# Exchanging the order of the grouped-attention projections in a hybrid encoder trunk

## The chip, the cores and the metric

The kernel runs on one core of a Trainium2 chip. The metric is the device time of one execution in microseconds, the median of several runs. The engines of the core work at the same time, each through a queue of its own in the order of the program: TensorE (PE, matmuls and transposes), VectorE (DVE), ScalarE (ACT), GpSimd (POOL) and SyncE (SP, which only starts transfers here). An instruction that waits for another engine holds up everything behind it in its own queue.

## What is computed

Two layers over 512 prompt tokens and 256 sample tokens of width 1024. Cut to what matters:

```python
def _layer(x, c, ...):
    hid = _rms_norm(x, norm_g) * (1.0 + scale) + shift
    qa, ka, va, za, qb, kb, vb, zb, ga, gb = split(hid @ w_in)
    oa = _neighbourhood_attention(qa, ka, va, rpb)       # 8 heads of 64
    ya = (oa * silu(za)) @ w_pa
    qh = _axial_rope(_rms_norm(qb, q_norm_g))            # 8 query heads of 64
    kh = _axial_rope(_rms_norm(kb, k_norm_g))            # 2 key heads of 64
    ob = _gqa_attention(qh, kh, vb)
    yb = (ob * silu(zb)) @ w_pb
    g_a, g_b = split(sigmoid(concat([ga, gb]) + b_gate))
    return x + gate * ((g_a * ya + g_b * yb) @ w_out)
```

## The kernel before

**Numbers.** Every float32 operand of a matmul is split into a high part (rounded, on ACT) and a low part (the rest, on DVE), and a product is three matmuls: high by high, low by high, high by low. Weights come as tiles of 128 x 1024 (`raw`, from `wst`, in the order in which they are used) and are split by `split_one` into `whi` and `wlo` (lines 222 and 228); `ahead` splits the first tiles of the next chunk of weights during the present one, and `need_unit` calls whatever split is still open.

**Steps.** All work inside a layer is written as a list of steps (`step`, line 153). A step issues a group of matmuls: six over 512 columns or twelve over 256. Then the step counter goes up, the functions that were put off to this number with `defer` are issued, and after them, from the list `slots`, as many entries as the rate allows: `rate[0]` is added to a credit at every step, and each whole credit issues one entry. The order of every engine's queue is thus fixed by hand: matmuls of the step, deferred work, slots.

**Attention in slots.** Attention is spread over the projections' steps. A neighbourhood head (`na_slots`, line 747) covers 17 slots and the heads start 8 slots apart; a head's transposes of its sample probabilities and its prompt product are in its slot 10, its sample product in slot 14. A grouped head (`gqa_slots`, line 885) covers 24 slots, and the heads start 12 apart, 108 slots in all. In a grouped head, counted from its first slot: scores of five tiles at slots 0, 2, 4, 6, 8; the row maximum one slot later on DVE (`gss`, line 915), the exponential two later on ACT (`gp`, line 925), the division three later (a reciprocal on DVE, line 937, then a product on POOL, line 939). The probabilities are transposed by PE into `gtp` (line 950) at slots 7, 8, 12, 13 and 17 and read out by ACT and DVE (lines 712, 717).

**Order of chunks in a layer.** The list `order` (line 1006): `va`, four `pair` chunks (queries and keys of two neighbourhood heads each), then `qb` (grouped queries, 24 steps) and `kvb` (grouped keys and values, 12 steps), then `za` (two chunks), four times `ga` and `pa`, then the same for branch B and the output projection. From the fourth `pair` on, the remaining neighbourhood slots are spread over `RQ` = 31 steps. At the end of `qb` and `kvb` any left are issued at once.

**Between the pairs and `za`.** At line 1302 the gains and the rotation table are loaded (`gn`, `tr`), and four products on DVE (line 1310) make from them one table of two halves for queries, `tabs[0]`, and one for keys, `tabs[1]`. A projection's result is squared and copied out by ACT (`rope_part`, lines 1323 and 1324), summed by DVE one step later (line 1327, `qss`) and rotated by POOL two steps later (lines 1332 to 1336). `rope_finish` (line 1342) takes the inverse roots by Newton steps on DVE, twelve small operations in two consecutive steps (lines 1350 to 1369, `ny`, `na`), and from the second step after multiplies them in (line 1363, `rr`).

While `roping[0]` is true, the neighbourhood heads' division runs on DVE (line 796) instead of POOL.

The constants in `SC` place what follows, in steps: `QF`, `QT`, `QTT` set when the roots of the prompt's queries are taken and when their four transposes (`q_tr_p`, `qt`, line 1391) start after the fourth query tile's read-out, and how far they are apart; `QS` and `QST` the same for the sample's (`q_tr_s`, line 1404). `KF` and `KT` count from the end of `kvb`: roots of the keys (`kfin`), transposes of the prompt's keys (`ktr(0)`, `kt`, line 1444), and, two steps on, of the sample's (`ktr(1)`). Each transposed tile is read out of PSUM by ACT (high part, `GQ` at line 680 or `GK` at lines 688 and 689) and by DVE one step later (low part, lines 681, 692, 693); for keys the second head one step after the first. All transposes, the attention's too, go through the PSUM pool `ps_t`, which has two buffers (line 78).

`kv_evac` (line 1419) also writes the values' table `vg`: two pairs of a high part on ACT and a low part on DVE. `vg` comes from the pool `vp`, which has two buffers, held until then by the neighbourhood values of heads 0 to 3 and 4 to 7.

`SGQ` steps after the end of the projections `start_gqa` (line 1519) puts the 108 slots into the list, at `len(slots) / SC["RG"]` a step. What is left of them when branch B begins is issued at once (line 1533).

Of the kernel before, what the change touches and what calls it, by code (L numbers as in the profile page):

```python
# [7 lines left out]
F32 = mybir.dt.float32  # L8
# [27 lines left out]
    RN=11.6,  # L36
    RQ=31,

    QF=4,
    QT=10,  # L40
    QTT=2,
    QS=5,
    QST=13,
    KF=5,
    KT=12,
    SGQ=15,
    RG=84,

    SR0=90,
    SR1=40,  # L50
# [10 lines left out]
def trunk(ctx: ExitStack, tc: tile.TileContext, xT, xq, wst, wad, wsd, vec, gain, trig, mask, eye, rpb, yT):  # L61
# [49 lines left out]
    def pitch(ap):  # L111
        return ap.ap[0]
# [8 lines left out]
    def galloc(shape, dtype, name):  # L121
        tag = free.pop(0)
        t = genp.tile(shape, dtype, tag=tag, name=name)
        owner[id(t)] = (tag, t)
        return t

    def gfree(t):
        tag, _ = owner.pop(id(t))
        free.append(tag)
# [12 lines left out]
    def defer(k, fn):  # L142
        later.setdefault(step_no[0] + k, []).append(fn)
# [540 lines left out]
    def evac_k(Kh, Kl, hp, src, sl):  # L684
        p0 = 64 * hp
        p1 = 64 - p0
        h = Kh[p0:p0 + 64, sl]
        A.activation(out=h, in_=src[p0:p0 + 64], func=AF.Copy)
        A.activation(out=Kh[p1:p1 + 64, sl], in_=src[p0:p0 + 64], func=AF.Copy)

        def low():
            V.tensor_sub(out=Kl[p0:p0 + 64, sl], in0=src[p0:p0 + 64], in1=h.bitcast(F32))
            V.tensor_sub(out=Kl[p1:p1 + 64, sl], in0=src[p0:p0 + 64], in1=h.bitcast(F32))

        defer(1, low)
# [51 lines left out]
    def na_slots(l, h, base, Q, Kh, Kl, v4, dst, on_done, first):  # L747
# [95 lines left out]
            st["o"] = o  # L843

        def pv_s():
            o = ps_o.tile([128, NP], F32, tag="o", name="os")
            n = 0
            for b in range(2):
                for pt in st["pt", 2]:
                    mm(o[:, 0:256], v4[:, 4 + b, hi4, :], pt[:, b, :], n == 0, n == 3)  # L850
                    n += 1
            st["o"] = o
# [136 lines left out]

    bms = {}  # L990
    roping = [False]
    GQ = []
    GK = []
    slots_abs = []
# [11 lines left out]
    for l in range(DEPTH):  # L1006
        order += [("va", l)]
        order += [("pair", l, p) for p in range(4)]
        order += [("qb", l), ("kvb", l)]
        order += [("za", l, 0), ("za", l, 1)]  # L1010
        for i in range(4):
            order += [("ga", l, i), ("pa", l, i)]
        order += [("zb", l, 0), ("zb", l, 1)]
        for i in range(4):
            order += [("gb", l, i), ("pb", l, i)]
        order += [("wo", l, i) for i in range(4)] + [("wor", l, i) for i in range(2)]
# [5 lines left out]
    def nxt(name):  # L1022
        assert todo.pop(0) == name, name

    with tc.manual_schedule():
# [213 lines left out]
        for l in range(DEPTH):  # L1239
# [19 lines left out]
            slots_abs.clear()  # L1259
            pushed[0] = 0  # L1260
            slot_base = 0
            rate[0] = 16 / SC["RN"]
            bms[l, 0] = bm_build(l, 0)
            for p in range(4):
# [38 lines left out]
            S.dma_start(out=gn, in_=gain[l].unsqueeze(0).to_broadcast([128, 4, 64]))  # L1303
            tr = galloc([128, 6, 2, 64], F32, "tr")
            S.dma_start(out=tr, in_=trig)
            tabs = []
            for w in range(2):
                tb = galloc([128, 6, 2, 64], F32, "tab")
                for s in range(2):
                    V.tensor_mul(out=tb[:, :, s, :], in0=tr[:, :, s, :],  # L1310
                                 in1=gn[:, 2 * w + s].unsqueeze(1).to_broadcast([128, 6, 64]))
                tabs.append(tb)
            gfree(gn)
            gfree(tr)

            GQ[:] = [None] * 8
            GK.clear()
# [1 line left out]
            def rope_part(src, tab, r, ss):  # L1319

                n, nh = src.shape[1], src.shape[2]
                sq = galloc([128, n, nh, 64], F32, "rsq")
                A.activation(out=sq, in_=src, func=AF.Square)
                A.activation(out=r, in_=src, func=AF.Copy)

                def part2():
                    V.tensor_reduce(out=ss, in_=sq, axis=AX.X, op=ALU.add)

                def part3():
                    for e in range(2):  # L1330
                        sb = tab[:, :, 1, 32 * e:32 * e + 32].unsqueeze(2)
                        G.tensor_mul(out=sq[:, :, :, 32 * e:32 * e + 32], in0=r[:, :, :, 32 - 32 * e:64 - 32 * e],
                                     in1=sb.to_broadcast([128, n, nh, 32]))
                    cb = tab[:, :, 0, :].unsqueeze(2).to_broadcast([128, n, nh, 64])
                    G.tensor_mul(out=r, in0=r, in1=cb)
                    G.tensor_add(out=r, in0=r, in1=sq)
                    gfree(sq)

                defer(1, part2)
                defer(2, part3)  # L1340

            def rope_finish(rs, ss):
# [18 lines left out]
                for i, r in enumerate(rs):  # L1361
# [2 lines left out]
                        out=r, in0=r, in1=yv[:, t:t + k, :].unsqueeze(3).to_broadcast([128, k, nh, 64])))  # L1364
                    t += k

            nxt(("qb", l))
            roping[0] = True
            qr = {}
            qss = smp.tile([128, 6, 8], F32, tag="qss8", name="qss", bufs=1)  # L1370

# [26 lines left out]
            def q_tr_s(w):  # L1398
# [9 lines left out]
                if w == 1:  # L1408
                    for j in (4, 5):
# [1 line left out]

            wide_pass(("qb", l), [(0, 1), (2,), (3,), (4, 5)], q_evac,
                      lambda i: ps_acc.tile([128, NP], F32, tag="acc", name="accw"))
            nxt(("kvb", l))
            kr = galloc([128, 6, 2, 64], F32, "rr")
            kss = smp.tile([128, 6, 2], F32, tag="qss2", name="qss", bufs=1)
            vg = vp.tile([128, 6, 4, 128], F32R, tag="v", name="vg")

            def kv_evac(b, acc):
                rope_part(acc[:, :, 0:128].rearrange("p t (h d) -> p t h d", d=64), tabs[1][:, 2 * b:2 * b + 2],  # L1420
                          kr[:, 2 * b:2 * b + 2],
                          kss[:, 2 * b:2 * b + 2, :])
                base = vg[:, 2 * b:2 * b + 2]
                pp = pitch(base)
                src = acc[:, :, 128:256].rearrange("p t (k d) -> p t k d", d=64)
                for e in range(2):
                    hi = bass.AP(base.tensor, base.offset + 192 * e, [pp, [512, 2], [256, 2], [1, 64]])
                    lo = bass.AP(base.tensor, base.offset + 64 + 64 * e, [pp, [512, 2], [256, 2], [1, 64]])
                    A.activation(out=hi, in_=src, func=AF.Copy)
                    V.tensor_sub(out=lo, in0=src, in1=hi.bitcast(F32))  # L1430

            token_chunk(("kvb", l), kv_evac)
            roping[0] = False

            def kfin():
                rope_finish([kr[:, 0:4], kr[:, 4:6]], kss)

            def ktr(g):
                c, n = RNG[g]
                if g == 0:  # L1440
                    GK.extend([[galloc([128, NT], F32R, "GK") for _ in range(2)] for _ in range(2)])
                t = ps_t.tile([128, n], F32, tag="t", name="kt")
                for j in range(n // 128):
                    T.transpose(t[:, 128 * j:128 * j + 128], kr[:, 4 * g + j].rearrange("p h d -> p (h d)"), ident)
                evac_k(GK[0][0], GK[0][1], 0, t, slice(c, c + n))
                defer(1, lambda: evac_k(GK[1][0], GK[1][1], 1, t, slice(c, c + n)))
                if g == 1:
                    gfree(kr)
                    gfree(tabs[1])

            defer(SC["KF"], kfin)
            defer(SC["KT"], lambda: ktr(0))
            defer(SC["KT"] + 2, lambda: ktr(1))


            oaz = {}
# [44 lines left out]
            for h in range(8):  # L1501
                if h % 2 == 0:
                    pr = h // 2

                    def alloc_ob(pr=pr):
                        ob[pr] = galloc([128, NT], F32, "ob")
                    while len(slots_abs) <= 12 * h:
                        slots_abs.append([])
                    slots_abs[12 * h].insert(0, alloc_ob)

                def gdn(h=h):
                    gfree(GQ[h])
                    if h % 4 == 3:
                        gfree(GK[h // 4][0])
                        gfree(GK[h // 4][1])

                gqa_slots(12 * h, h, vg, ob, gdn)

            def start_gqa():
                push_slots()  # L1520
# [202 lines left out]
def _layout(inputs):  # L1723
# [33 lines left out]
    for l in range(DEPTH):  # L1757
        w = w_in[l]
        st += wide(w[:, va])
        for p in range(4):  # L1760
            st += halves(np.concatenate([cols(w, qa, p, 128), cols(w, ka, p, 128)], axis=1))
        st += wide(hperm(w[:, qb]))
        st += halves(np.concatenate([hperm(w[:, kb]), w[:, vb]], axis=1))
        for i in range(2):
            st += halves(cols(w, za, i))
        for i in range(4):
            st += halves(cols(w, ga, i))
            st += halves(g["w_pa"][l][:, 256 * i:256 * i + 256])
        for i in range(2):
            st += halves(cols(w, zb, i))  # L1770
        for i in range(4):
            st += halves(cols(w, gb, i))
            st += halves(g["w_pb"][l][:, 256 * i:256 * i + 256])
        for i in range(4):
            st += halves(g["w_out"][l][:, 256 * i:256 * i + 256])
        st += st[-8:-4]
# [80 lines left out]
```

## Time and profile before

| | before |
|---|---|
| median of 3 runs | 1226.61 us (1225.98 to 1226.78) |
| the profiled execution | 1225.67 us |
| its span, first to last instruction | 1223.9 us |
| ACT busy | 579.7 us (47%) |
| POOL busy | 342.9 us (28%) |
| mean granted TensorE clock | 0.997 |

The span is what the profile's rows add up in; the rest of the execution's time lies around it. In a row of the timeline stand the start, the duration, the engine, the line, the operation, `written<-read`, the shapes and a count; in brackets the idle time before it and what ended it. Busy time of PE is modelled at the ends of matmuls, which overlap, so a matmul's share is read from the distance of starts. In a row of windows stand the stretch, its length, and the busy time of PE, PEld (weight loads), DVE, ACT and POOL with instruction counts, then the granted clock, the DMA engines' share and GB/s.

### The profile page before, as it was taken

How to read it: one execution, taken by the hardware profiler on the slowest of the kernel's cores; microseconds unless marked ns; L12 is line 12 of the kernel's file. 1: busy time of each engine (PE TensorE's matmuls, PEld its weight loads, DVE VectorE, ACT ScalarE, POOL GpSimd, SP SyncE). 2: the span in 40 equal slices, each digit the busy share in tenths (PEclk: the TensorE clock that was granted, in tenths of full speed). 3: DMA queues.
4: the chain of work that ended last, by engine and by line, in shares of the span. 5: the costliest groups of instructions: out<-in, count | busy, mean ns of one | idle time of the engine just before them, and what ended most of it. 6: DMA issues, size and time to landing. Idle time of an engine off the chain costs nothing.

```text
span 1223.9 us, 19495 instructions
## 1 busy us (share of the span) xinstructions
PE 1202.9 (98%) x7276; PEld 1056.5 (86%) x7276; DVE 816.6 (67%) x1609; ACT 579.7 (47%) x1229; POOL 342.9 (28%) x382
## 2 busy tenths in 40 slices
PE   8999999999999999999999999999999999999997
PEld 5789989889898988887888998898898998888886
DVE  5757887875556458998484788777656554763536
ACT  4547755465555332433154676555545543332323
POOL 0025454442223121121131443554222212211102
PEclk9999999999999999999999999999999999999998
DMA  9443411111111235566443233111111112431424
GB/s 344 150 126 86 118 55 52 52 52 36 35 36 52 70 105 154 174 185 197 139 151 109 75 92 109 35 48 57 31 40 53 36 52 87 146 95 52 129 95 155
DMA packets 48125, 118.28 MB, mean 97 GB/s; under 512 B 5408, under 2 KB 11936, under 8 KB 48032
## 3 DMA queue, kind: packets, MB, share of 16 engines
q1 hardware_dynamic: 47888, 116.98, 30.9%
q8 instruction: 57, 0.93, 0.3%
q14 instruction: 36, 0.29, 0.1%
q10 hardware_dynamic: 144, 0.07, 0.0%
HBM read 110.74 MB, written 6.29 MB: 96 GB/s over the span
## 4 chain that ended last, share of the span: by engine, by line
PE 81%; DVE 10%; ACT 4%; issue 2%; DMA 2%; POOL 0%; SPq 0%; DVEq 0%; ACTq 0%; POOLq 0%
PE accp L115 37%; PE accs L115 19%; PE accw L115 9%; PE go L115 3%; PE gsp L115 3%; PE gtp L950 3%; PE acct L115 2%; DVE wlo L228 2%; ACT p L788 1%; PE sp L115 1%; DVE GQ L681 1%; DMA adaraw<-in_wad 1%; PE op L115 1%; PE adat L115 1%; DVE ptl L717 1%
## 5 line engine op out<-in xcount | busy, mean ns | idle before, releaser
L115 PE MATMUL accp<-hh,whi 128*128 128x512 f32 x512 | 203.4, 397 | 0.0
L115 PE MATMUL accp<-hl,whi 128*128 128x512 f32 x512 | 200.1, 391 | 0.0
L115 PE MATMUL accp<-hh,wlo 128*128 128x512 f32 x512 | 199.8, 390 | 0.0
L228 DVE TENSOR_TENSOR wlo<-raw,whi 128x1024 fp32r<-128x1024 f32 x119 | 158.5, 1333 | 53.5 <-ACT whi L222 52.9
L115 PE MATMUL accs<-hh,whi 128*128 128x256 f32 x512 | 145.9, 285 | 0.0
L115 PE MATMUL accs<-hh,wlo 128*128 128x256 f32 x512 | 144.8, 283 | 0.0
L115 PE MATMUL accs<-hl,whi 128*128 128x256 f32 x512 | 144.8, 283 | 0.0
L939 POOL TENSOR_TENSOR gp<-gp,gss 128x512 f32<-128x512 f32 x80 | 83.1, 1040 | 210.4 <-DVE gss L937 169.4
L222 ACT ACTIVATE whi<-raw 128x1024 fp32r<-128x1024 f32 x124 | 129.4, 1054 | 16.8 <-PE accw L115 8.2
L115 PEld LDWEIGHTS accp<-hh,wlo 128*128 128x128 f32 x512 | 96.1, 188 | 20.8
L115 PEld LDWEIGHTS accp<-hh,whi 128*128 128x128 f32 x512 | 96.4, 188 | 17.8
L115 PEld LDWEIGHTS accp<-hl,whi 128*128 128x128 f32 x512 | 96.4, 188 | 17.1
L115 PEld LDWEIGHTS accs<-hl,whi 128*128 128x128 f32 x512 | 97.9, 191 | 1.0
L115 PEld LDWEIGHTS accs<-hh,whi 128*128 128x128 f32 x512 | 97.9, 191 | 0.9
L115 PEld LDWEIGHTS accs<-hh,wlo 128*128 128x128 f32 x512 | 97.9, 191 | 0.0
L712 ACT ACTIVATE pth<-gtp 128x512 fp32r<-128x512 f32 x80 | 47.8, 598 | 100.6 <-PE go L115 83.5
L456 DVE SCALAR_TENSOR_TENSOR adaacc<-adaraw,csil,adaacc 128x512 f32<-128x512 f32 x112 | 88.6, 851 | 3.2 <-DMA adaraw<-in_wsd 3.1
L1567 POOL TENSOR_TENSOR th<-th 128x512 f32<-128x512 f32 (+1 forms) x32 | 42.4, 1338 | 167.7 <-DVE th L1560 167.7
L735 POOL TENSOR_TENSOR bm<-u,masks 128x128 f32<-128x128 f32 (+2 forms) x80 | 40.4, 529 | 162.3 <-DMA u<-in_rpb 162.3
L717 DVE TENSOR_TENSOR ptl<-gtp,pth 128x512 fp32r<-128x512 f32 x80 | 54.7, 685 | 39.9 <-ACT pth L712 39.3
L915 DVE TENSOR_REDUCE gss<-gsp 128x1 f32<-128x512 f32 x64 | 43.8, 685 | 51.9 <-PE gsp L115 51.6
L115 PE MATMUL accw<-whi,hh 128*128 128x512 f32 x192 | 77.3, 403 | 0.0
(244 smaller groups left out, 2991.3 us busy)
## 6 DMA issues: line engine op xcount, KB each, us to landing
raw<-in_wst SPq DMA_DIRECT2D x124, 512.0 KB, 3.6
adaraw<-in_wsd SPq DMA_DIRECT2D x64, 256.0 KB, 3.1
adaraw<-in_wad SPq DMA_DIRECT2D x32, 256.0 KB, 5.9
u<-in_rpb SPq DMA_DIRECT2D x16, 354.5 KB, 4.8
u<-in_rpb SPq DMA_DIRECT2D x16, 236.5 KB, 4.4
out_y<-y SPq DMA_DIRECT2D x12, 256.0 KB, 2.5
x<-in_xT SPq DMA_DIRECT2D x8, 256.0 KB, 5.4
res<-in_xT SPq DMA_DIRECT2D x8, 256.0 KB, 4.2
```

The costliest lines, as they stand in the source:

```text
L115: T.matmul(out=out, lhsT=lhsT, rhs=rhs, start=start, stop=stop, skip_group_check=True)
L222: A.activation(out=hi, in_=r, func=AF.Copy)
L228: eng.tensor_sub(out=lo, in0=r, in1=hi.bitcast(F32))
L456: V.scalar_tensor_tensor(out=acc[n, h, g], in0=r, scalar=c, in1=acc[n, h, g], op0=ALU.mult, op1=ALU.add)
L681: defer(1, lambda h=h, lo=lo, s=s: V.scalar_tensor_tensor(out=lo, in0=s, scalar=scale, in1=h.bitcast(F32), op0=ALU.mult, op1=ALU.subtract))
L712: A.activation(out=h, in_=t, func=AF.Copy)
L717: V.tensor_sub(out=lo, in0=t, in1=h.bitcast(F32))
L735: G.tensor_tensor(out=o.rearrange("p (c r) -> p c r", r=r), in0=u, in1=mk.rearrange("p (c r) -> p c r", r=r), op=ALU.add)
L915: V.tensor_reduce(out=ss[:, 0:1], in_=sp, axis=AX.X, op=ALU.max, negate=True)
L939: G.tensor_mul(out=pv_, in0=pv_, in1=ss[:, 4:4 + n].unsqueeze(2).to_broadcast([128, n, w]))
L950: T.transpose(t[:, q, 128 * j:128 * j + 128], src, ident)
L1567: G.tensor_add(out=t[:, sl], in0=t[:, sl], in1=mrg[k][:, sl])
```

## The change

The chunk `kvb` stands before `qb`, in `order`, in the program and in the layout of the weights. The four products of the tables become four deferred pieces, at steps 2, 4, 6 and 8 after the pairs, the keys' two first. The placing constants change. Grouped attention's slots start 5 steps after the projections' end instead of 15 and are spread over 94 steps instead of 84. A counter, `v_left`, makes sure that the sample products of heads 0 to 3 have been issued before `vg` is allocated, by issuing slots if need be; `vg` is then kept in the list `vgs`. `roping[0]` is set at the start of `kvb` and cleared at the end of `qb`.

```diff
-    QF=4,
-    QT=10,
+    QF=3,
+    QT=9,
     QTT=2,
-    QS=5,
-    QST=13,
+    QS=3,
+    QST=8,
     KF=5,
     KT=12,
-    SGQ=15,
-    RG=84,
+    SGQ=5,
+    RG=94,
...
         def pv_s():
+            if h < 4:
+                v_left[0] -= 1
             o = ps_o.tile([128, NP], F32, tag="o", name="os")
...
-        order += [("qb", l), ("kvb", l)]
+        order += [("kvb", l), ("qb", l)]
...
+            v_left[0] = 4
             rate[0] = 16 / SC["RN"]
...
-            tabs = []
-            for w in range(2):
-                tb = galloc([128, 6, 2, 64], F32, "tab")
-                for s in range(2):
-                    V.tensor_mul(out=tb[:, :, s, :], in0=tr[:, :, s, :],
-                                 in1=gn[:, 2 * w + s].unsqueeze(1).to_broadcast([128, 6, 64]))
-                tabs.append(tb)
-            gfree(gn)
-            gfree(tr)
+            tabs = {}
+
+            def tab_piece(w, s):
+                if s == 0:
+                    tabs[w] = galloc([128, 6, 2, 64], F32, "tab")
+                V.tensor_mul(out=tabs[w][:, :, s, :], in0=tr[:, :, s, :],
+                             in1=gn[:, 2 * w + s].unsqueeze(1).to_broadcast([128, 6, 64]))
+                if w == 0 and s == 1:
+                    gfree(gn)
+                    gfree(tr)
+
+            for n, (w, s) in enumerate(((1, 0), (1, 1), (0, 0), (0, 1))):
+                defer(2 + 2 * n, lambda w=w, s=s: tab_piece(w, s))
...
+            nxt(("kvb", l))
+            roping[0] = True
...
+                if b == 0:
+                    while v_left[0]:
+                        slot_one()
+                    vgs.append(vp.tile([128, 6, 4, 128], F32R, tag="v", name="vg"))
...
+            token_chunk(("kvb", l), kv_evac)
...
+            defer(SC["KF"], kfin)
+            defer(SC["KT"], lambda: ktr(0))
+            defer(SC["KT"] + 2, lambda: ktr(1))
+
             nxt(("qb", l))
-            roping[0] = True
...
             wide_pass(("qb", l), [(0, 1), (2,), (3,), (4, 5)], q_evac,
                       lambda i: ps_acc.tile([128, NP], F32, tag="acc", name="accw"))
-            nxt(("kvb", l))
...
-            token_chunk(("kvb", l), kv_evac)
             roping[0] = False
...
+        st += halves(np.concatenate([hperm(w[:, kb]), w[:, vb]], axis=1))
         st += wide(hperm(w[:, qb]))
-        st += halves(np.concatenate([hperm(w[:, kb]), w[:, vb]], axis=1))
```

The parts of `kvb` left out here (`rope_part` on the keys, the pairs of `vg`, `kfin`, `ktr`) are moved as they are.

More of the change, by code (lines that the diff above doesn't have):

```diff
@@ L991, in trunk @@
     roping = [False]
+    v_left = [0]
     GQ = []
@@ L1365, in rope_finish, with kv_evac, kfin, ktr @@
                     t += k
+            nxt(("kvb", l))
+            roping[0] = True
+            kr = galloc([128, 6, 2, 64], F32, "rr")
+            kss = smp.tile([128, 6, 2], F32, tag="qss2", name="qss", bufs=1)
+            vgs = []
+            def kv_evac(b, acc):
+                rope_part(acc[:, :, 0:128].rearrange("p t (h d) -> p t h d", d=64), tabs[1][:, 2 * b:2 * b + 2],
+                          kr[:, 2 * b:2 * b + 2],
+                          kss[:, 2 * b:2 * b + 2, :])
+                if b == 0:
+                    while v_left[0]:
+                        slot_one()
+                    vgs.append(vp.tile([128, 6, 4, 128], F32R, tag="v", name="vg"))
+                base = vgs[0][:, 2 * b:2 * b + 2]
+                pp = pitch(base)
+                src = acc[:, :, 128:256].rearrange("p t (k d) -> p t k d", d=64)
+                for e in range(2):
+                    hi = bass.AP(base.tensor, base.offset + 192 * e, [pp, [512, 2], [256, 2], [1, 64]])
+                    lo = bass.AP(base.tensor, base.offset + 64 + 64 * e, [pp, [512, 2], [256, 2], [1, 64]])
+                    A.activation(out=hi, in_=src, func=AF.Copy)
+                    V.tensor_sub(out=lo, in0=src, in1=hi.bitcast(F32))
+            token_chunk(("kvb", l), kv_evac)
+            def kfin():
+                rope_finish([kr[:, 0:4], kr[:, 4:6]], kss)
+            def ktr(g):
+                c, n = RNG[g]
+                if g == 0:
+                    GK.extend([[galloc([128, NT], F32R, "GK") for _ in range(2)] for _ in range(2)])
+                t = ps_t.tile([128, n], F32, tag="t", name="kt")
+                for j in range(n // 128):
+                    T.transpose(t[:, 128 * j:128 * j + 128], kr[:, 4 * g + j].rearrange("p h d -> p (h d)"), ident)
+                evac_k(GK[0][0], GK[0][1], 0, t, slice(c, c + n))
+                defer(1, lambda: evac_k(GK[1][0], GK[1][1], 1, t, slice(c, c + n)))
+                if g == 1:
+                    gfree(kr)
+                    gfree(tabs[1])
+            defer(SC["KF"], kfin)
+            defer(SC["KT"], lambda: ktr(0))
+            defer(SC["KT"] + 2, lambda: ktr(1))
             nxt(("qb", l))
-            roping[0] = True
             qr = {}
@@ L1413, in trunk @@
                       lambda i: ps_acc.tile([128, NP], F32, tag="acc", name="accw"))
-            nxt(("kvb", l))
[L1415 to L1430, printed above, removed]
-            token_chunk(("kvb", l), kv_evac)
-            roping[0] = False
[L1435 to L1453, printed above, removed]
+            roping[0] = False
             oaz = {}
@@ L1515, in gdn @@
                         gfree(GK[h // 4][1])
-                gqa_slots(12 * h, h, vg, ob, gdn)
+                gqa_slots(12 * h, h, vgs[0], ob, gdn)
             def start_gqa():
```

## The prediction

> **What bounds the kernel now.** First the page's head, then busy time by stages, then what PE waited for.
>
> ```profile
> span 1223.9 us, 19495 instructions
> PE 1202.9 (98%) x7276; PEld 1056.5 (86%) x7276; DVE 816.6 (67%) x1609; ACT 579.7 (47%) x1229; POOL 342.9 (28%) x382
> ```
>
> TensorE works for 1202.9 of 1223.9 us, and the change neither adds nor removes a matmul. So all it can move is PE's waiting. The windows show the stages that the diff touches, layer 0 first: 65 us with the grouped projections (`qb`, `kvb`), then 40 us in which grouped attention starts.
>
> ```profile
> 155.00:220.00 65.00, 63.78 (x402) 56.88 (x401) 50.33 (x118) 35.35 (x77) 34.61 (x37) 1.00 0.20 59
> 220.00:260.00 40.00, 37.13 (x216) 32.22 (x215) 35.05 (x69) 22.66 (x50) 17.95 (x19) 1.00 0.18 54
> 748.00:813.00 65.00, 63.79 (x402) 56.88 (x402) 49.75 (x116) 35.23 (x77) 34.84 (x38) 1.00 0.19 58
> 813.00:853.00 40.00, 37.12 (x216) 32.23 (x215) 34.89 (x68) 22.75 (x51) 18.12 (x19) 1.00 0.19 54
> ```
>
> The first number after the comma is PE's, the third VectorE's (DVE). PE idles 1.22 + 2.87 us in layer 0 and 1.21 + 2.88 in layer 1: 8.18 us in all. In the second stage DVE is busy 35.05 of 40 us: there it sets the pace. The list of waits names PE's stops, each once per layer (total of both, count, longest):
>
> ```profile
> PE kt L1444 <- DVE rr L1363: 3.1, 2, 1.6
> PE gsp L115 <- ACT gp L925: 2.6, 2, 1.3
> PE op L115 <- DVE ptl L717: 2.0, 2, 1.0
> ```
>
> The rest of the 8.18 are two stops of 0.1 us per layer. Around a stop PE also restarts late:
>
> ```profile
> 165.11 0.39 PE L115 MATMUL op<-ptl,v 128*128 128x256 f32 x1 [1.00 <-DVE ptl L717]
> 165.33 0.28 PE L115 MATMUL op<-pth,v 128*128 128x256 f32 x1
> ```
>
> The next matmul starts 0.22 us later where 0.12 is usual (below), and the idle time is counted from a modelled end. I add 0.2 us for each of five stops, an estimate: 4.1 + 1.0 = **5.1 us a layer**, 10.2 in all, is the most the change can win; 1215 us is its floor.
>
> **The change part by part.** Count steps from the end of the last pair. Emission at step n is reached by PE when n steps of matmuls are out. Step costs:
>
> ```profile
> 1143.76 43.86 PE accp L115 x192
> 424.82 5.75 PE accs L115 x48
> 199.64 0.60 PE L809 MATMUL tp<-ident,p 128*128 128x128 f32 x4
> 200.00 0.36 PE L115 MATMUL acct<-whi,hh 128*128 128x256 f32 x1
> ```
>
> A matmul over 512 columns costs 0.228 us, over 256 0.12, four transposes 0.35 (their results are there after 0.6). A step is 6 x 0.228 = 1.37 or 12 x 0.12 = 1.44 us, plus slots and transposes.
>
> *Tables in pieces.* Now the four products stand together in front of the first slots' work:
>
> ```profile
> 159.18 1.97 DVE L1310 TENSOR_TENSOR tab<-tr,gn 128x384 f32<-128x384 f32 x4
> 161.06 1.22 DVE L228 TENSOR_TENSOR wlo<-raw,whi 128x1024 fp32r<-128x1024 f32 x1
> 163.25 1.21 DVE L228 TENSOR_TENSOR wlo<-raw,whi 128x1024 fp32r<-128x1024 f32 x1
> 164.38 0.68 DVE L717 TENSOR_TENSOR ptl<-tp,pth 128x512 fp32r<-128x512 f32 x1
> ```
>
> The `ptl` that PE waits for ends at 165.06, behind 1.97 us of tables and 2.43 us of weight splits. Afterwards a piece (0.49) comes every second step, and `kvb` has two weight tiles, not four, so its next splits come from its third and sixth step. That `ptl` is ready about 2.7 us earlier (1.5 of tables, one split): the 1.0 us stop goes. The second, 0.1 us stop at step 24 goes too, since the query roots that precede it move to steps 32 and 33. No new stop in steps 0 to 12: the `vg` pairs (0.39 ACT, 0.42 DVE, twice each, three times) fill what the splits leave. Bounds 0 to 1 us; I take 0. The guard `v_left` costs nothing: slot 66 on step 24 at 27/31 a step means that 46 slots are out before step 1, and the fourth head's sample product is slot 38, so no slot is forced.
>
> *Keys first.* `kfin` moves from step 41 to 17, `ktr` from 48 and 50 to 24 and 26. The 1.55 us stop at `kt` goes. But `kt` now meets the last neighbourhood slots:
>
> ```profile
> 239.87 0.59 ACT L688 ACTIVATE GK<-kt 64x512 fp32r<-64x512 f32 x1 [0.21 <-PE kt L1444]
> 241.09 0.68 DVE L692 TENSOR_TENSOR GK<-kt,GK 64x512 fp32r<-64x512 f32 x1 [0.50 <-ACT GK L689]
> 245.21 0.69 DVE L693 TENSOR_TENSOR GK<-kt,GK 64x512 fp32r<-64x512 f32 x1
>   ACT GK L688: 0.4, 1
> ```
>
> The last head's sample transposes stand right behind step 24 (the rows `tp` and first `acct` of layer 0 above), hence between the two `kt`, and `ps_t` has two buffers. So the second `kt` must wait until the first is read out: 0.6 + 2 x 0.59 ACT + 2 x 0.69 DVE, and the same for the other key head, 5.8 us from its issue. PE gets there after the first `kt` 0.35, the head's products 8 x 0.12, `tp` 0.35 and two steps 2 x 1.37: 4.4. The wait is 1.4 us if ACT's second pair waits for DVE's first, as the last row (who waited for `GK`) has it once, and 0 if not. I take **1.0**.
>
> *Queries last, attention at step 41 instead of 51.* Slots run at 108/94 = 1.149 a step (was 1.286), so slot 0 falls on step 41, 4 on 45, 5 on 46, 6 and 7 on 47. Prompt transposes `q_tr_p` fall on 38, 40, 42, 44, the sample ones on 45 and 47. Set 0 at step 37. PE reaches step 45 after 7 x 1.37 + 1.44 + 4 x 0.35 + two scores of 0.46 = 13.35 us. At 45 the transposes need the buffer of the third prompt pair, so DVE must have read it. DVE's queue up to there, by these rows:
>
> ```profile
> 200.61 0.68 DVE L1327 TENSOR_REDUCE qss<-rsq 128x8 f32<-128x512 f32 x1
> 213.55 1.39 DVE L681 SCALAR_TENSOR_TENSOR GQ<-qt,GQ 64x512 fp32r<-64x512 f32 x2
> 219.47 0.69 DVE L1363 TENSOR_TENSOR rr<-rr,ny 128x512 f32<-128x512 f32 x1
> 239.91 0.68 DVE L1468 SCALAR_TENSOR_TENSOR zt<-zt,accp 128x512 f32<-128x512 f32 x1
> 217.50 0.18 DVE L368 TENSOR_TENSOR na<-na,qss 128x16 f32<-128x16 f32 x1
> 217.71 0.60 DVE L369 SCALAR_TENSOR_TENSOR ny<-na,ny 128x16 f32<-128x16 f32 x1
> 205.03 1.20 ACT L680 ACTIVATE GQ<-qt 64x512 fp32r<-64x512 f32 x2 [3.03 <-PE qt L1391]
> 206.75 1.43 POOL L1332 TENSOR_TENSOR rsq<-rr,tab 128x256 f32<-128x256 f32 x2
> 209.61 1.30 POOL L1336 TENSOR_TENSOR rr<-rr,rsq 128x512 f32<-128x512 f32 x1
> ```
>
> One `rr` of the prompt 0.69, two reduces 1.36, three pairs of `GQ` 4.17, two `wlo` 2.44, twelve Newton operations at 0.21 from start to start 2.5, two `rr` of the sample 1.38, `zt` 0.68, the row maximum `gss`, a reduce of the same size, 0.68: 13.9. DVE also idles 1.5 us: its first three are done at 1.7, and the first `GQ` is there at 1.37 + 0.6 + 1.20 = 3.2. It is done at 15.4, so PE waits **2.1 us** at least. The upper end: POOL rotates the sample queries from 1 to 10 (twice 1.43 + 1.30 and a third operation of that size, 8.1 us), and beside such work every second Newton operation took 0.60 for 0.18. Six so slowed make 2.5 us more: 4.6. I take **2.4**, near the lower end: it goes by the whole list of rows, the upper one by this one spot.
>
> The Trainium skill ("SBUF — State Buffer", Who interferes with whom) has the port that GpSimd shares with VectorE's second SBUF input as an exclusive lock, the later one blocked for the whole instruction. By it most Newton operations would be slowed, and the upper end, 4.6, would hold. The trace agrees in part: 0.18 and 0.60 alternate.
>
> Next, step 47 transposes the first two probability tiles. The second needs `norm(1)` (slot 5), queued on DVE behind the sample queries' low parts:
>
> ```profile
> 226.25 1.54 ACT L680 ACTIVATE GQ<-qt 64x256 fp32r<-64x256 f32 x4
> 227.82 1.73 DVE L681 SCALAR_TENSOR_TENSOR GQ<-qt,GQ 64x256 fp32r<-64x256 f32 x4 [0.68 <-ACT GQ L680]
> 242.06 0.63 ACT L1478 ACTIVATE zh<-zt 128x512 fp32r<-128x512 f32 x1 [1.00 <-POOL zt L1471]
> 239.31 0.68 DVE L1482 TENSOR_TENSOR zl<-zt,zh 128x512 fp32r<-128x512 f32 x1
> 253.23 0.15 DVE L937 RECIPROCAL gss<-gss 128x1 f32<-128x1 f32 x1
> 257.75 1.04 POOL L939 TENSOR_TENSOR gp<-gp,gss 128x512 f32<-128x512 f32 x1 [1.30 <-DVE gss L937]
> ```
>
> From the transposes at 45: 0.6 + 1.54 + 0.63 + 0.68 + 1.73 + 0.68 + 0.15 + 1.04 = 7.0 us. PE arrives after 0.35 + 0.46 + 2 x 1.44 + 0.35 + 0.46 + 0.1 = 4.6. The wait is **2.4**; without `zh` and `zl` in the way, 1.1.
>
> The old `gsp` stop (1.3) goes: `rowmax` no longer queues behind `GK`. Thinner slots later win nothing, as PE has no stop in the list between 260 us and the end of the branch; the leftover of 3 slots is the same (92 x 1.149 against 82 x 1.286, both 105 of 108). DMAs and their order on SP are the same but for two exchanged weight chunks.
>
> **Sum.** Per layer 1.0 + 2.4 + 2.4 = 5.8 new against 5.1 old: +0.7, twice, +1.4 us. The profiled execution took 1225.67 (its span 1223.9, the rest lies around it): 1227.1. The median of the runs shown is 0.94 above it: **1228.0**.
>
> **The rivals.**
> - *DVE keeps up* (faster). The new waits need its queue to be full by step 43; should it lag 2 us less, the first falls to 0.4, the second to 1.1, `kt` to 0.6: 2.1 against 5.1, so 6 us less, 1221. For it: DVE loses the key work from this stage (twelve Newton operations, two `rr`, eight `GK`, about 8 us by the rows above). Against it: the first head's five row maxima, five reciprocals and reads of `gtp` come in, about as much.
> - *POOL blocks DVE* (slower). 4.6 + 2.5 + 1.4 and 0.7 at step 48 (the buffer of the last sample transposes): 9.2 against 5.1, +8.2, 1234.8. It decides once the third pair's low parts end later than about 16.3 on the scale above.
> - *The tables free nothing*: the `op` stops stay, behind the pair's own low parts. +1.2 a layer on the forecast: 1230.4. Against it: 2.7 us gained where 1.0 is needed.
> - *The clock falls.* In the last stage, with 4.47 us idle, the granted clock is 0.91; with 1.55 us of idling it stays 1.00:
>
> ```profile
> 220.00:240.00 20.00, 18.45 (x111) 16.16 (x110) 17.69 (x39) 8.38 (x19) 7.71 (x9) 1.00 0.16 49
> 1200.00:1220.00 20.00, 15.53 (x124) 14.86 (x122) 14.03 (x31) 8.11 (x16) 3.81 (x3) 0.91 0.55 190
> ```
>
> If the wait at step 45 reaches the 4.6 us of the upper end and the clock then falls as there, 9% of 20 us is 1.8 us more a layer: 1238.4. The Trainium skill ("TensorE: Matmul & The Clock Gate", Part 1: The HAM clock gate) sets the limit at an idle window of about 3.4 us; by that rule the forecast's 2.4 leaves the clock alone.
>
> **How the numbers follow.** A measurement of this kernel can tell about 0.2% (2.4 us) from no change: 1224.2 to 1229.1 is "same". Chances: forecast 0.40; DVE keeps up 0.27; POOL blocks 0.25; tables 0.05; clock 0.03. The first rival spreads from 1217 to 1224, the second from 1229 to 1235. The range 1220.5 to 1233 leaves out a third of each and the last. The likeliest case alone: 1224.2 to 1229.1.
>
> **What would show it.** The waits of PE on `op` and on `kt` for `rr` are gone. In their place stand `kt` waiting for DVE `GK`, sample `qt` waiting for DVE `GQ`, `gtp` for POOL `gp`. If none of these passes 0.5 us, the first rival holds and my queue is too long; if `qt` passes 3.5, the second. A stop in steps 0 to 12, or anywhere outside the two stages, would be one I haven't seen.

## The result and the profile after

The changed kernel takes 1237.74 us (median of 4 runs, 1235.83 to 1238.67) against 1226.30 for the kernel before beside it: a ratio of 1.0092 (95% interval 1.0080 to 1.0103), so about 11.4 us slower. The profiled execution took 1238.63 us, 12.96 more than the profiled one of before. Line numbers below are those of each run's own kernel; in the changed kernel moved code stands up to some fifty lines from its old place.

The head of the page after, then its windows over the stretches that were shown of before, with one of the first `kvb` steps in front. The stretches are fixed times: in layer 1 the changed kernel reaches the same work some 7 us later.

```profile
span 1236.8 us, 19473 instructions
PE 1207.8 (98%) x7276; PEld 1061.1 (86%) x7276; DVE 812.0 (66%) x1609; ACT 580.6 (47%) x1229; POOL 347.3 (28%) x382
```

```profile
160.00:180.00 20.00, 20.00 (x165) 19.74 (x164) 16.61 (x42) 10.83 (x32) 7.43 (x13) 1.00 0.19 53
...
155.00:220.00 65.00, 63.69 (x402) 57.13 (x401) 50.29 (x128) 37.05 (x86) 33.00 (x38) 1.00 0.21 59
220.00:260.00 40.00, 32.78 (x178) 28.27 (x177) 30.81 (x56) 21.75 (x46) 19.14 (x17) 0.91 0.13 40
...
813.00:853.00 40.00, 32.80 (x177) 27.94 (x176) 34.43 (x68) 21.50 (x44) 17.24 (x16) 0.96 0.18 53
```

The first stage loses as much as it did: PE idles 1.31 us of 65 (1.22 before). The second has got worse in both layers: 7.22 and 7.20 us idle of 40 where it was 2.87 and 2.88, and the granted clock there is 0.91 and 0.96 where it was 1.00. The list of PE's waits (total, count, longest) names the stops:

```profile
PE qt L1455 <- DVE GQ L681: 10.3, 2, 5.2
PE kt L1408 <- DVE GK L693: 2.6, 2, 1.3
PE gtp L952 <- DVE GQ L681: 2.5, 2, 1.7
PE gtp L952 <- POOL gp L941: 1.6, 2, 1.3
```

They are the places that the prediction named. One of them is twice as long as its number: the sample queries' transposes stand 5.2 us in each layer. PE's timeline around it in layer 0, one row of layer 1, where the same transposes start at 839.09, and the clock in the 7 us that follow in each:

```profile
239.62 1.08 PE L1455 MATMUL qt<-ident,rr 128*128 128x128 f32 x4 [5.17 <-DVE GQ L681]
...
241.36 0.41 PE L115 MATMUL accs<-hh,whi 128*128 128x256 f32 x1
...
245.94 0.60 PE L1455 MATMUL qt<-ident,rr 128*128 128x128 f32 x4
...
252.00 0.48 PE L115 MATMUL accp<-hh,whi 128*128 128x512 f32 x1
...
850.50 0.48 PE L115 MATMUL accp<-hh,whi 128*128 128x512 f32 x1
```

```profile
239.00:246.00 7.00, 6.38 (x31) 6.21 (x32) 5.65 (x11) 3.41 (x8) 1.04 (x1) 0.55 0.17 64
...
839.00:846.00 7.00, 6.52 (x37) 5.96 (x37) 5.73 (x12) 4.31 (x11) 1.27 (x2) 0.76 0.11 44
```

After the wait TensorE runs at about half its clock, for some 6 us in layer 0 and some 3 us in layer 1. In layer 0 the 24 `accs` matmuls from 241.36 to 245.94 take 4.58 us where 24 x 0.12 = 2.88 is usual, and the four transposes and the scores ahead of them 1.74 where the next such pair takes about 0.9: 2.5 us that no list of waits shows. In layer 1 the same two take 3.67 (840.77 to 844.44) and 1.68: 1.6 us.

What was DVE doing meanwhile? Its timeline in layer 0, and POOL's beside it (its first row and its last are the neighbours of that rotation):

```profile
225.13 1.59 DVE L228 TENSOR_TENSOR wlo<-raw,whi 128x1024 fp32r<-128x1024 f32 x1
226.65 0.71 DVE L1358 TENSOR_SCALAR qss<-qss 128x16 f32<-128x16 f32 x1
227.39 0.67 DVE L361 TENSOR_SCALAR ny<-qss 128x16 int32<-128x16 int32 x1
228.09 0.17 DVE L363 TENSOR_SCALAR ny<-ny 128x16 int32<-128x16 int32 x1
228.30 1.14 DVE L367 SCALAR_TENSOR_TENSOR na<-ny 128x16 f32<-128x16 f32 x1
229.47 0.17 DVE L368 TENSOR_TENSOR na<-na,qss 128x16 f32<-128x16 f32 x1
229.68 1.16 DVE L369 SCALAR_TENSOR_TENSOR ny<-na,ny 128x16 f32<-128x16 f32 x1
...
235.55 1.91 DVE L228 TENSOR_TENSOR wlo<-raw,whi 128x1024 fp32r<-128x1024 f32 x1
237.38 0.68 DVE L1371 TENSOR_TENSOR rr<-rr,ny 128x512 f32<-128x512 f32 x1
238.09 1.39 DVE L681 SCALAR_TENSOR_TENSOR GQ<-qt,GQ 64x512 fp32r<-64x512 f32 x2
```

```profile
224.35 1.28 POOL L1344 TENSOR_TENSOR rr<-rr,rsq 128x512 f32<-128x512 f32 x1
225.60 2.42 POOL L1340 TENSOR_TENSOR rsq<-rr,tab 128x256 f32<-128x256 f32 x2
228.10 1.31 POOL L1343 TENSOR_TENSOR rr<-rr,tab 128x512 f32<-128x512 f32 x1
229.49 1.32 POOL L1344 TENSOR_TENSOR rr<-rr,rsq 128x512 f32<-128x512 f32 x1
235.11 1.26 POOL L1483 TENSOR_TENSOR zt<-zt,oa 128x512 f32<-128x512 f32 x1 [4.30 <-DVE zt L1480]
```

The six small operations of the roots' first step take from 226.65 to 230.84: 4.2 us instead of the 1.25 of six operations at 0.21. POOL rotates the sample queries at that time, and the long ones end where a POOL instruction ends (228.0, 229.4, 230.8). The two `wlo`, 1.22 us long when alone, end about 1.1 us after a POOL instruction's end (225.6, 236.4): the first is 0.37 us longer, the second 0.69. The last row of DVE is what PE waits for: the third prompt pair's low parts, ended at 239.48 behind two `wlo` and the last `rr`.

### The profile page after: what moved, and what is told of

Its sections match the earlier page's. It is cut to its first block, busy times and chain, and to the rows that moved or that the text cites. A ratio compares the mean times of both kernels' runs of the same rounds, so it can differ in the third digit from the quotient of the medians.

```text
span 1236.8 us, 19473 instructions
## 1 busy us (share of the span) xinstructions
PE 1207.8 (98%) x7276; PEld 1061.1 (86%) x7276; DVE 812.0 (66%) x1609; ACT 580.6 (47%) x1229; POOL 347.3 (28%) x382
## 4 chain that ended last, share of the span: by engine, by line
PE 91%; DVE 5%; DMA 1%; ACT 1%; issue 1%; POOL 0%; DVEq 0%; ACTq 0%
PE accp L115 40%; PE accs L115 20%; PE accw L115 10%; PE go L115 3%; PE acct L115 3%; PE gtp L952 3%; PE gsp L115 3%; PE sp L115 2%; PE op L115 1%; DVE GQ L681 1%; PE adat L115 1%; PE junk L115 1%; DMA raw<-in_wst 1%; PE os L115 1%; DVE wlo L228 1%
## 5 line engine op out<-in xcount | busy, mean ns | idle before, releaser
L941 POOL TENSOR_TENSOR gp<-gp,gss 128x512 f32<-128x512 f32 x80 | 85.9, 1073 | 236.3 <-DVE gss L939 221.9
L115 PE MATMUL accw<-whi,hl 128*128 128x512 f32 x192 | 75.5, 393 | 0.0
```

The source lines that it names most:

```text
L115: T.matmul(out=out, lhsT=lhsT, rhs=rhs, start=start, stop=stop, skip_group_check=True)
L941: G.tensor_mul(out=pv_, in0=pv_, in1=ss[:, 4:4 + n].unsqueeze(2).to_broadcast([128, n, w]))
```

## The experiments

All ratios are against the kernel before, run beside on the same chip, with a 95% interval. "Before" took 1226.06 (first four), 1226.38 (next three) and 1225.88 us (last three).

**e1_tables: the tables in pieces, alone.** The kernel before, with its four products deferred, the queries' first.

```diff
+            for n, (w, s) in enumerate(((0, 0), (0, 1), (1, 0), (1, 1))):
+                defer(2 + 2 * n, lambda w=w, s=s: tab_piece(w, s))
```

> The kernel before with one part of the change alone: the four table products at steps 2, 4, 6 and 8 (queries' first, since qb is first here). If the products held up the neighbourhood head's low part, PE's wait on op for ptl (1.0 us a layer, 1.2 with its restart) goes: 1223.9 us against 1226.3. If the pair's own low parts and the weight splits were enough to cause it, no change, 1226.3.

Measured 1224.43 us, ratio 0.9986 (0.9977 to 0.9995). Its PE waits:

```profile
PE kt L1448 <- DVE rr L1367: 3.1, 2, 1.5
...
PE op L115 <- DVE ptl L717: 0.6, 2, 0.3
```

The `op` stop falls from 1.0 to 0.3 us, the other two (`kt` 1.5, `gsp` 1.3) stay. This part works and is worth about 1.6 us.

**e2_consts: the change with the old placing constants.**

```diff
-    QF=3,
-    QT=9,
+    QF=4,
+    QT=10,
...
-    QS=3,
-    QST=8,
+    QS=5,
+    QST=13,
...
-    SGQ=5,
-    RG=94,
+    SGQ=15,
+    RG=84,
```

> The changed kernel with the placing constants of before (QF 4, QT 10, QS 5, QST 13, SGQ 15, RG 84): exchanged order and table pieces stay. If the constants make the loss (the sample queries' transposes fall on step 45, when VectorE is full), PE's wait of 5.2 us on qt goes, the second kt still waits 1.3 us, and the time is 1219 to 1222 us. If the exchanged order makes it, it stays above 1230.

Measured 1225.09 us, ratio 0.9990 (0.9981 to 0.9999). So the constants make all of the loss (12.6 us), and the exchanged order, with the tables in pieces, stands 0.7 us above e1_tables: by itself it wins nothing. Its expected time, 1219 to 1222, was missed by 3 us, because the scores now wait 2.2 and 0.3 us a layer where they waited 1.3. PE's waits, and then rows of DVE at the same roots:

```profile
PE gsp L115 <- ACT gp L927: 4.9, 4, 2.2
PE kt L1408 <- DVE GK L693: 2.6, 2, 1.3
```

```profile
228.26 0.66 DVE L363 TENSOR_SCALAR ny<-ny 128x16 int32<-128x16 int32 x1
...
229.17 1.16 DVE L368 TENSOR_TENSOR na<-na,qss 128x16 f32<-128x16 f32 x1
```

The wait at `qt` is gone although DVE's small operations are held up here too. The sample transposes come 8 steps after their roots (13 - 5) instead of 5 (8 - 3), and three steps are over 4 us of slack.

**e3_norot: no POOL work at that place.** The change, with POOL's rotation of the two sample query tiles taken out: the sample queries stay unrotated.

```diff
-                    for e in range(2):
+                    for e in range(2) if rot else ():
...
-                    G.tensor_mul(out=r, in0=r, in1=cb)
-                    G.tensor_add(out=r, in0=r, in1=sq)
+                    if rot:
+                        G.tensor_mul(out=r, in0=r, in1=cb)
+                        G.tensor_add(out=r, in0=r, in1=sq)
...
+                           rot=i < 4)
```

> The changed kernel without POOL's rotation of the two sample query tiles (the sample queries stay unrotated). Theory 1, POOL blocks VectorE: the Newton operations fall from up to 1.16 us to 0.2, VectorE reaches the third pair's low parts some 4 us earlier, the wait on qt falls from 5.2 to 1 to 2 us, the granted clock in 220 to 260 us stays 1.00, time about 1226. Theory 2, there is too much VectorE work in steps 37 to 45: the wait stays above 4 us and the time above 1234.

Measured 1228.97 us, ratio 1.0020 (1.0011 to 1.0030): 8.8 us come back. One group of the roots in the grouped lines of both kernels, 216 to 252 us, first the changed kernel, then this one, then its waits:

```profile
L369 DVE SCALAR_TENSOR_TENSOR ny<-na,ny 128x16 f32<-128x16 f32 x3 | 1.5, 502 | 0.1
```

```profile
L369 DVE SCALAR_TENSOR_TENSOR ny<-na,ny 128x16 f32<-128x16 f32 x3 | 0.5, 174 | 0.1
```

```profile
PE qt L1457 <- DVE GQ L681: 3.7, 2, 1.9
PE gtp L952 <- POOL gp L941: 3.2, 2, 1.6
```

Without the rotation no small operation is held up, the wait falls from 5.2 to 1.9 us, and the clock in the second stage is 1.00 again. The rows account for all of it: the first six operations take 1.21 us instead of 4.20, and the first `wlo` 1.22 instead of 1.59, together 3.36, and the wait is 3.31 shorter. The 1.9 that are left stand close to the prediction's lower bound (2.1), although the second `wlo` still takes 1.93 beside POOL's `zt`. The time is 3 us above the 1226 expected; the waits on `gtp`, which grow from 2.05 to 2.5 us a layer, are about 1 us of that.

**e4_kt: the keys' transposes in another PSUM pool.**

```diff
-                t = ps_t.tile([128, n], F32, tag="t", name="kt")
+                t = ps_acc.tile([128, n], F32, tag="acc", name="kt")
```

> The changed kernel with the two kt tiles taken from the accumulators' pool ps_acc (three buffers) instead of ps_t. If the second kt waits for a ps_t buffer, its 1.3 us (1.5 with the restart) a layer go and nothing takes their place: 1234.8. If VectorE is the bound up to step 45, what PE gains at kt it loses at qt: 1237.7, with the wait on qt grown to 6.6 us.

Measured 1236.78 us, ratio 1.0089 (1.0075 to 1.0103). Of its waits:

```profile
PE qt L1455 <- DVE GQ L681: 10.3, 2, 5.2
...
PE qt L1442 <- DVE GQ L681: 1.0, 2, 0.5
PE accw L115 <- DVE GK L693: 0.7, 2, 0.4
```

The `kt` stop is gone, but 0.4 us return at the accumulators `accw`, which now wait for a buffer that `kt` holds, and 0.5 at the prompt's `qt`; the sample's wait is as long as before. So 1.7 of the 2.6 us come back as other stops, and neither of the two expected cases came whole. The 1 us that the median lies below the changed kernel fits that, but the runs spread from 1234.8 to 1239.8.

**e5_busy: a wait filled with work.** The change, with 20 more matmuls over 512 columns, all of zeros, in front of the sample's first `qt`: TensorE isn't idle there.

```diff
+                if w == 0:
+                    bz = ps_o.tile([128, NP], F32, tag="o", name="busy")
+                    for _ in range(20):
+                        mm(bz, cst, cst.unsqueeze(1).to_broadcast([128, 4, 128]), True, True)
```

> The changed kernel with 20 idle matmuls over 512 columns (4.6 us, zeros, into the buffer of the output products, unused then) right ahead of the first sample qt, so that PE works through most of its 5.2 us of waiting. The wait on qt falls to about 0.6 us and the granted clock stays 1.00 in 220 to 260 us. Theory 1, the fallen clock costs its full 2.6 us a layer (24 matmuls of 256 columns took 4.58 us instead of 2.88, and 0.9 before them): about 1232.5. Theory 2, the next thing due after the sample transposes is set by the chain ACT, VectorE, POOL (7.0 us to the second probability transpose) and not by PE: the wait on gtp for gp grows from 0.3 and 1.3 us to about 2.4, and the time is 1236 to 1237.

Measured 1236.81 us, ratio 1.0085 (1.0068 to 1.0102). Its waits and its second stage in layer 1:

```profile
PE gtp L952 <- POOL gp L941: 3.2, 2, 1.6
...
PE gtp L952 <- DVE GQ L681: 1.5, 3, 0.5
PE qt L1459 <- DVE GQ L681: 1.2, 2, 0.6
```

```profile
813.00:853.00 40.00, 36.85 (x201) 30.74 (x200) 35.23 (x70) 21.98 (x46) 18.03 (x18) 1.00 0.17 53
```

The clock holds in layer 1; in layer 0 it holds up to 246 us and falls behind that (0.66 from 246 to 251), so the stage has 0.96. The time falls by 0.9 us, where theory 1 asked for 5.2; it is in theory 2's range, though the wait on `gtp` for `gp` is 1.6 us and not 2.4. How much the slow clock costs is read from one stretch that the changed kernel, e3_norot and this one have in common, from the sample's first `qt` to the first `accp` behind the eighth `gtp`: 12.38 us in layer 0 of the changed kernel (239.62 to 252.00), 11.41 in its layer 1 (839.09 to 850.50), and 10.61 here in layer 1 (838.18 to 848.79), where the clock is full; in e3_norot, with the full clock too, 10.60 (235.58 to 246.18) and 10.61 (830.40 to 841.01). So of the 2.5 and 1.6 us that the matmuls lose, about 1.8 and 0.8 lengthen the kernel; the other 0.8 in each layer are made up behind, mostly at the waits on `gtp`, which are 2.05 us a layer there and 2.5 with the full clock.

**e6_place and e7_place_kt: other constants for the changed order.** The first takes the sample's roots three steps later, so that less of POOL's rotation runs beside them, and starts attention four steps later; the second also moves the second `kt` by two steps.

```diff
-    QS=3,
-    QST=8,
+    QS=6,
+    QST=10,
...
-    SGQ=5,
-    RG=94,
+    SGQ=9,
+    RG=90,
```

```diff
-            defer(SC["KT"] + 2, lambda: ktr(1))
+            defer(SC["KT"] + 4, lambda: ktr(1))
```

> The changed kernel with four constants only: sample roots at QS 6 instead of 3 (step 43, after POOL's rotation), sample transposes at QST 10 instead of 8 (steps 47 and 49), attention from SGQ 9 instead of 5 over RG 90 steps instead of 94. If the loss is that the Newton operations lie beside POOL's rotation and the transposes come due before VectorE is through, the wait on qt falls below 0.5 us, the clock stays 1.00, and the time is 1219 to 1223 us with kt's 1.5 a layer and some 1 to 2 us a layer on gsp or gtp left. If VectorE has too much work in steps 37 to 49 wherever it stands, waits of 4 us or more a layer remain and the time is above 1228.

> As e6_place, and the second kt two steps later (step 28 instead of 26), when the first one's buffer has been read out. If kt's wait goes by itself and VectorE has room behind it: 3 us below e6_place. If VectorE is the bound at attention's start, the same time as e6_place, and the waits there grow by what kt gave.

Measured 1237.92 us, ratio 1.0092 (1.0077 to 1.0107), and 1238.33, ratio 1.0098 (1.0083 to 1.0114). The waits of e6_place, its clock after the first of them, and the wait of e7_place_kt:

```profile
PE qt L1455 <- DVE rr L1371: 5.8, 4, 2.3
PE gsp L115 <- ACT gp L927: 3.6, 2, 1.8
```

```profile
240.00:244.00 4.00, 4.00 (x18) 3.58 (x17) 2.72 (x7) 1.80 (x5) 1.92 (x2) 0.57 0.00 0
```

```profile
PE qt L1455 <- DVE rr L1371: 7.6, 4, 2.3
```

The hoped-for case of e6_place failed; its time is that of the other case (above 1228), but not for the reason given there. The roots moved, but `QST` of 10 leaves four steps after them (eight with the old constants), and the transposes now wait for their own data, `rr`, instead of for a buffer; the scores wait 1.8 us after that. Later, at 301 and 344 us in layer 0 and again in layer 1, `go` waits 0.7 and 0.6 us for DVE, which the changed kernel doesn't. In e7_place_kt PE doesn't stop at `kt` (65.00 us busy of 65), and `qt` waits 0.9 us more a layer: PE only arrives earlier at the same VectorE.

**e8_late_attn: early sample transposes, late attention.**

```diff
-    SGQ=5,
-    RG=94,
+    SGQ=15,
+    RG=84,
```

> The changed kernel with attention's start and rate of before (SGQ 15, RG 84), the query constants as changed: the sample transposes still fall on steps 45 and 47. If these alone make the loss, coming five steps after their roots and beside POOL's rotation, the wait on qt stays near 5.3 us, the clock falls, and the time is 1231 to 1236. If attention's early start makes it (its row maxima on VectorE, its scores on PE), the wait on qt falls below 3 us and the time is near that with all constants of before, 1225.

Measured 1233.04 us, ratio 1.0060 (1.0046 to 1.0074). Its waits:

```profile
PE qt L1455 <- DVE GQ L681: 9.9, 2, 4.9
```

The changed query constants alone keep the long wait. Against e2_consts the kernel differs in the four constants of the queries alone: 1233.04 - 1225.09, about 8 us. Starting attention ten steps earlier costs the rest of the loss, 1237.74 - 1233.04 or about 5 us, the `gtp` waits among them.

**e9_tables_pw and e10_consts_pw: work from DVE to POOL.** To e1_tables and e2_consts: the four low parts of `za`'s weights on POOL.

```diff
-    PW=("wor01", "wor11", "va3"),
+    PW=("wor01", "wor11", "va3", "za00", "za01", "za10", "za11"),
```

> The kernel before with the tables in pieces and the four low parts of za's weights on POOL instead of VectorE (5 us of VectorE's work, 2.5 us each on POOL). If VectorE's load between steps 36 and 56 is the bound, the waits on kt (1.5 us a layer) and gsp (1.3) shrink by more than half: 1220 to 1222 us. If POOL's work beside it only slows VectorE's operations with two inputs in SBUF, or the weights' low parts come late for PE: 1224 or more, with a wait of za's matmuls on POOL wlo.

> The same edit on the changed kernel with the constants of before (exchanged order, tables in pieces). VectorE as the bound: the wait on gsp (2.2 and 0.3 us a layer) shrinks by more than half, kt's 1.3 stays: 1220 to 1222. Otherwise 1225 or more.

Measured 1230.64 us, ratio 1.0035 (1.0022 to 1.0049), and 1232.62, ratio 1.0048 (1.0036 to 1.0061): 6.2 and 7.5 us above their bases. In e9_tables_pw DVE and POOL stand like this, and PE waits so in the two kernels:

```profile
228.62 2.32 DVE L367 SCALAR_TENSOR_TENSOR na<-ny 128x12 f32<-128x12 f32 x1
230.97 2.33 DVE L368 TENSOR_TENSOR na<-na,qss 128x12 f32<-128x12 f32 x1
```

```profile
228.51 4.75 POOL L228 TENSOR_TENSOR wlo<-raw,whi 128x1024 fp32r<-128x1024 f32 x2
```

```profile
PE gsp L115 <- ACT gp L925: 5.7, 2, 2.9
```

```profile
PE gsp L115 <- ACT gp L927: 8.2, 2, 4.1
```

Two splits on POOL take 4.75 us, and each holds up one tiny DVE operation for its whole length. At these two DVE gives away 1.22 us of work a split and stands 2.15 us (2.32 - 0.17) for it; and the scores' wait on the chain DVE, POOL, ACT grows from 1.3 to 2.9 us, in the other kernel from 2.2 to 4.1. The profiled execution of e9_tables_pw took 1228.35 us; there the longer wait makes 3.0 of the 3.8 us above e1_tables' profiled one. What makes the other 2.3 us of the median isn't shown.

## Why the prediction was wrong

The prediction was 1228.0 us, in 1220.5 to 1233; the three rivals that lie above it (POOL blocks DVE, the tables free nothing, the clock falls) had 0.33 together. The places of all stops were right. What failed is the size of one term, the wait at step 45 (2.4 taken, 5.2 measured), and the fall of the clock that follows from it.

- **Tables in pieces** (1.0 us a layer): right. The `op` stop is not among the waits after, PE is busy 20.00 of 20 us from 160 to 180, and e1_tables wins with it alone.
- **Keys first** (the `rr` wait at `kt` goes, one on DVE `GK` comes, 0 to 1.4, taken 1.0): mechanism right, 1.3 measured. The exchange gives back at `kt` nearly all that it wins there.
- **The wait at step 45** (2.1 to 4.6, taken 2.4): here the forecast failed. PE was ready at 234.3 us, half a microsecond after the forecast's 13.35; DVE at 239.48 against 15.4, that is 235.9 on the same scale (its zero, step 37, at 220.5). The wait measured 5.2, above the upper end too. The queue that I wrote down was the right one; its durations weren't. (Its first three operations, "done at 1.7", add up to 2.05 by the rows given there, so the lower bound should have been about 1.7; that is small beside the rest.) The roots' first six operations took 2.9 us more than reckoned, the two `wlo` 3.50 instead of 2.44; the rest made up 0.4. I took the lower end because it went "by the whole list of rows", but the 0.21 of its twelve Newton operations is the spacing at one that no POOL instruction held up. The upper end was short because it priced a slowed operation by the one example at hand, 0.60 for 0.18 at 217.71, and that stood beside the rotation of a tile half as wide; it also left the `wlo` at 1.22. POOL's timeline of the kernel before:

```profile
217.51 0.77 POOL L1335 TENSOR_TENSOR rr<-rr,tab 128x256 f32<-128x256 f32 x1
```

  That POOL instruction takes 0.77 us, the ones of the sample queries 1.31, and the operations held up by them 1.14 and 1.16. The price belonged to POOL's instruction, and the 1.30 was among the prediction's own rows. e3_norot shows the cause: without the rotation the wait is 1.9. The prediction's own sign, `qt` passing 3.5, had named this rival.
- **The wait at step 47** (2.4): right in size, 2.05 us idle a layer after, but more than half of it stands on the low parts `GQ` of the sample (2.5 of 4.1 us for both layers), which I had as one part of the chain only. The size is partly luck: PE came there late, at the slow clock; with the full clock, in e3_norot, these waits make 2.5.
- **The clock** (0.03; 1.8 us a layer if the wait reached 4.6): the condition was met. The matmuls lost 2.5 us in layer 0 and 1.6 in layer 1, of which about 1.8 and 0.8 reached the time. The Trainium skill's limit ("TensorE: Matmul & The Clock Gate", Part 1: The HAM clock gate: an idle window of about 3.4 us) agrees with a fall after 5.2 us and none after the 1.9 of e3_norot. It doesn't cover e6_place, where the clock fell after 0.55 and 2.33 us within 3.2, so the forecast's 2.4 wasn't safe by this measurement. The chance was too low in any case: the wait that brings the fall had 0.25.
- **The rivals.** "POOL blocks DVE" (1234.8) was the true one, with its point of decision, 16.3, passed by 2.7, and the clock came on top as in the last rival (1238.4). That 1238.4 lies so near the 1237.74 is partly luck: the wait at step 45 was longer than in it, the clock's loss in layer 1 (0.8) and the terms at steps 47 and 48 (2.05 for 2.5 + 0.7) smaller.

The sum after, in layer 0: 1.3 at `kt`, 5.2 at `qt`, 2.5 of clock, 2.05 at `gtp` and about 0.5 of restarts (an estimate) make 11.6, against 5.1 before: 6.5. In layer 1, with 1.6 of clock, it is 5.6. (The prediction counted 1.0 of restarts among the old stops and none among the new ones: with its own 0.2 for each of three stops its sum stands 1.2 us higher.) Measured from the first `sp` of a layer to its last `go`, layer 0 takes 334.04 us instead of 327.70 and layer 1 333.05 instead of 327.66: 6.3 and 5.4 more, 11.7 together. The two profiled executions differ by 12.96; of the rest, 1.08 us were there before the first `sp`, ahead of everything that the change touches.

The Trainium skill's rule ("SBUF — State Buffer", Who interferes with whom), by which the later engine is blocked for the whole instruction, was put aside for "agrees in part: 0.18 and 0.60 alternate". The alternation was the rule's own sign: after each POOL instruction a DVE operation gets in, and the next one waits for the following POOL instruction. The rows of e9_tables_pw (2.32, 2.33 and POOL's 4.75 for two) agree with it to a tenth of a microsecond.

What stays open: why the slow clock lasted 6 us in one layer and 3 in the other after waits of the same length, and what e4_kt's freed `kt` is worth within a microsecond. No constants were found with which the exchanged order beats e1_tables, the fastest kernel of this study; not all were tried.

## What to carry to other kernels

Where work of GpSimd runs beside a row of small VectorE operations, count the GpSimd instructions in that stretch and charge VectorE up to the whole length of each; price such a spot by the neighbour's instruction, not by the small operation. Moving a deferred transpose nearer to its data takes away slack; here that cost about 8 us (e8_late_attn against e2_consts), in a stretch where the reading engine is nearly full (35 of 40 us in the kernel before). Splitting a burst of preparation into pieces between steps won 1.6 us, the only gain found here. A rival whose condition is another rival's outcome needs a chance that goes with it: the clock's fall had 0.03, the wait that brings it 0.25.

## What the hardware showed

- A VectorE operation on 128x16 elements takes 0.17 us alone and 1.14 to 1.16 us beside POOL's products and sums of 1.3 us, 2.32 us beside POOL's subtraction over 1024 columns (128x12 there). The forms with one array read (`qss`, `ny`, at 0.71 and 0.67) were held up as well as those with two.
- One wait of 5.2 us is followed by some 6 us at about half the clock in layer 0 (mean 0.55 over 7 us) and some 3 us in layer 1 (0.76 over 7 us). In e6_place two waits of 0.55 and 2.33 us within 3.2 us are followed by 0.57 over 4 us, so a stop need not be unbroken for the clock to fall.
